# A two-layer diffusion trunk on one core: the opening's mean, context columns and load plan, and the neighbourhood scores in one matmul

## The chip, the cores and the metric

The kernel runs on one core of a Trainium2 chip. The metric is the device time of one execution in microseconds (us), from start to end of the program. A core has engines that run side by side, each with its own queue of instructions: TensorE (PE, matrix multiplies; PEld is its weight load), VectorE (DVE), ScalarE (ACT), GpSimd (POOL) and SyncE (SP), which issues the transfers (DMA) from the main memory. Engines wait for one another by semaphores. Matmuls write to PSUM, eight banks of 512 float32 per partition; everything else lies in SBUF, 128 partitions wide.

## The reference, cut to what matters

```python
for l in range(DEPTH):                                   # DEPTH = 2, D_MODEL = 1024
    mod = silu_c @ w_mod[l] + b_mod[l]                   # 6 vectors of 1024 for the latent tokens
    mod_c = silu_cc @ w_mod[l] + b_mod[l]                # the same for the context tokens
    h = modulate(rms_norm(x, norm1[l]), sh1, sc1)        # 512 latent tokens
    hc = modulate(rms_norm(ctx, norm1[l]), csh1, csc1)   # 256 context tokens
    na_q, na_k, na_v, gq, gk, gv, ga, gb = jnp.split(h @ w_in[l], IN_SPLITS, axis=-1)
    ...                                                  # the same of hc @ w_in[l]
    ya = merge_heads(na_latent(qa, ka, va, ka_c, va_c, bias, row_idx))
    ...                                                  # yb: grouped-query attention
    x = x + g1 * branch_merge(ya, yb, ga, gb, w_pa[l], w_pb[l], w_o[l])
    ...                                                  # the context likewise, but not in the last layer
    h2 = modulate(rms_norm(x, norm2[l]), sh2, sc2)
    x = x + g2 * swiglu(h2, w_ffn_in[l], w_ffn_out[l])
return rms_norm(x, final_norm)

def rms_norm(x, g):
    y = x * lax.rsqrt(jnp.mean(x * x, axis=-1, keepdims=True) + EPS)
    return y * g

def na_latent(q, k, v, k_ctx, v_ctx, bias, row_idx):     # 8 heads, a window of 8 x 16 in a grid of 8 x 64
    s_win = jnp.einsum('bhrwd,bhrjud->bhrwju', qg, kg) * SCALE + bias[None]
    s_ctx = jnp.einsum('bhrwd,bhld->bhrwl', qg, k_ctx) * SCALE
    p = jax.nn.softmax(jnp.concatenate([s_win, s_ctx], axis=-1), axis=-1)
    ...
```

So the softmax of a latent query of the neighbourhood heads runs over its window of latent keys and all 256 context keys.

## The kernel before, in words

All activations are kept with features on the partitions: the 1024 features are eight blocks `k` of 128 partitions (`KB = 8`), and the 768 tokens are columns, 512 latent (`S`) and then 256 context (`T = 768`). Each float32 product is made of three matmuls on rounded halves: high by high, high by low, low by high.

**The opening** (`Trunk.start`, L812 on) computes the first layer's norm and modulation and the first three blocks of the input projection, `gk`, `gv` and `gq`, numbered `i` = 0, 1, 2. It is written as a list of operations with an engine, an estimated cost, what they come after, and an urgency (`Ops.add`). `Ops.run` (L554) puts them in an order by simulating the engines with these estimates, from a start time `START`, and issues them in this order for all engines; on PE, where its own simulation sees a gap, it puts in small matmuls without a use (`warm`, L836). What the list holds:

- `token` and `square`: load block k of x (eight loads, each 128x768), square it on ScalarE.
- `total` (L847): VectorE adds squares 1 to 6 onto square 0, six adds that form a chain; square 7 is kept apart.
- `means` (L853): per 128 tokens one matmul with a column of 1/1024, once for the summed tile and once for square 7, both into `st`.
- `eps`, `power`, `widen`: add epsilon, raise to -1/2 on GpSimd, spread the result over the partitions into `rb` by TensorE (L870).
- `fetch` (L631 in `raw`): the first layer's modulation weights `wmod`, two loads of 512 KB per block k, into nine buffers (`AHEAD`), so that a load from the tenth on waits for an earlier block's sums. `sums` (L891): 16 matmuls per block into a bank of the tag `m`. `parts` (L897): ScalarE copies the bank out. `choose` (L901): four small matmuls that sort the result. `settle` (L906, L909): VectorE finishes the block's scale and shift.
- `scaled`, `high`, `low` (L915, L920, L924): per block and span `s` (0: 512 latent columns, 1: 256 context columns) the modulated norm and its two rounded halves.
- `wraw`, `whigh`, `wlow`: load and split the weights of `gk`, `gv`, `gq` (`win`).
- `multiply` (L950): three matmuls per (i, s, k) into the bank of (i, s). There are three banks of the tag `a`. The banks are taken where a sum begins, so (0, 0), (1, 0), (2, 0) get one each, and a context sum (i, 1) waits until (i, 0) has been copied out: `prev = [out[i, 0]] if s else []`.

PSUM's eight banks in this stage are three for `a`, three for `n` (`ch`, `st`, `rb`) and two for `m`. The order of the loads is the string `FIRST`: the eight blocks of x, the small biases, then `0 w 1 2 w 3 w 4 5 6 7`, where a digit is a block of wmod and `w` a block of win. The loads of the next stage (`mixing`) are not in the list; the build places them into SP's queue by its own simulation.

**Attention** (`mixing`, L1658 on) runs pairs of query blocks as items, with the remaining projections as filler between them. In the first layer the order on PE is written out by `Flow`, from fixed costs per item; in the second layer `Plan` records all operations of all engines and puts them in order by its own simulation, with costs by the width of each operation (`cost`, L351). The latent tokens are sorted so that a block of 128 queries (16 columns of the grid) needs 256 neighbouring latent keys.

**Neighbourhood scores** (`na_pair`, L1424): for each of a head's four query blocks `b` there is one bank `s` of 512 scores: 256 latent keys, then 256 context keys. It is filled by matmuls with `q` as weights (high and low half, `hl`) and `k` as the moving operand: for b < 3 latent keys from 128 b on (256 columns) and the context keys (256). For b = 3 the window wraps around: latent keys 384 to 512 (128 columns), 0 to 128 (128), and the context (256). `soft` (L1441) adds the bias tile from `rpb` and finds the minimum, ACT takes the exponential. `turn` (L1456) transposes the 128x128 pieces for the product with the values; `to` is where a piece lands.

Of the kernel before, what the change touches and what calls it, by code (L numbers as in the profile page):

```python
# [3 lines left out]

# [85 lines left out]
HOWW = "vvv"  # L90
START, HOP, LAND = 4.06, 0.15, 0.25
SAME = dict(v=0.22, a=0.0, g=0.0, p=0.0)
# [511 lines left out]
class Trunk:  # L604
# [207 lines left out]
    def start(self, h, pool, others):  # L812
# [19 lines left out]
        add = todo.add  # L832
        chosen = self.ps("n", "ch")

        def warm():
# [10 lines left out]
        def total(k):  # L846
            nc.vector.tensor_tensor(sqs[0], sqs[0], sqs[k], op=ALU.add)  # L847

        def means(k):
            if k == 0:  # L850
                tiles["st"] = self.ps("n", "st")
            for t in range(nt):
                nc.tensor.matmul(  # L853
                    tiles["st"][:, t : t + 1], sqs[k][:, t * P : (t + 1) * P], self.ones, start=(k == 0 and t == 0),
                    stop=(k > 0), skip_group_check=True)

# [86 lines left out]
        def multiply(i, s, k):  # L943
            if k == 0:
                self.ahead[i, s] = self.ps("a", "pj")
# [11 lines left out]
        for what in FIRST.split():  # L957
            if what == "x":
                k = len(loaded)
                loaded.append(add("d", 0.92, token, (k,), [], 1))  # L960
                sq = add("a", 0.77, square, (k,), [loaded[k]], 1)
                if k < KB - 1:
                    last = add("v", 0.87, total, (k,), [last, sq], 1) if k else sq
                    continue
                last = add("p", 1.34, means, (0,), [last], 0)
                last = add("v", 0.08, eps, (), [add("p", 1.34, means, (KB - 1,), [last, sq], 0)], 0)
                wide = [
                    add("p", c, widen, (s,), [add("g", g, power, (s,), [last], 0)], 0)
                    for s, c, g in ((0, 0.86, 0.96), (1, 0.43, 0.63))]
            elif what == "w":  # L970
                i = len(wdone)
                hi = add("a", 0.97, whigh, (i,), [add("d", 1.26, wraw, (i,), [], 1)], 2.15 + 0.1 * i)
                eng = HOWW[i]
                wdone.append((hi, add(eng, 2.31 if eng == "g" else 1.13, wlow, (i, eng), [hi], 2.15 + 0.1 * i)))
            elif what == "b":
                bias = add("v", 0.35, biases, (), [add("d", 0.45, small, (), [], 1)], 0)
            else:
                k = int(what)
                at = []
                for half in range(2):  # L980
                    at.append(add("d", 1.26, fetch, (k, half), free[-AHEAD] if len(free) >= AHEAD else [], 1))
                    free.append([])
                run = add("p", 1.2, sums, (k,), at, 3 + 0.1 * k)
                for users in free[-2:]:
                    users.append(run)
                run = add("a", 0.4, parts, (k,), [run], 0)
                run = add("p", 0.5, choose, (k,), [run], 0)
                got[k] = add("v", 0.4, settle, (k,), [run, bias], 0)
        for t, n in ((self.cos, "cos"), (self.sin, "sin")):
# [3 lines left out]
        for k in range(KB):  # L993
            for s, (u, hi, lo) in enumerate(((0.68, 0.62, 0.68), (0.4, 0.4, 0.4))):
                t = add("v", u, scaled, (k, s), [wide[s], got[k], loaded[k]], 2 + k * 0.1)
# [3 lines left out]
        for s in range(2):  # L999
            for i in range(3):  # L1000

                prev = [out[i, 0]] if s else []
                for k in range(KB):
                    prev = [add("p", (0.7, 0.37)[s], multiply, (i, s, k), [*halves[k, s], *wdone[i], *prev], 4)]
                out[i, s] = add("a", (1.05, 0.6)[s], evac, (i,), prev, 1)
        everything = {mybir.EngineType[e] if hasattr(mybir.EngineType, "__getitem__") else getattr(mybir.EngineType, e)
# [417 lines left out]
    def na_pair(self, head, q, k, val, bias, out, i, pool, done=None):  # L1424
# [4 lines left out]
        def scores(s, b):  # L1429
            if b < 3:  # L1430
                parts = [(0, 256, P * b)]
            else:
                parts = [(0, P, P * b), (P, 256, 0)]
            parts.append((256, 512, S))
            for hl in range(2):
                for j, (lo, up, src) in enumerate(parts):
                    nc.tensor.matmul(
                        s[:, lo:up], q[hl][:, b * P : (b + 1) * P], k[:, src : src + up - lo],
                        start=(hl == 0 and j == 0), stop=(hl == 1 and j == len(parts) - 1), skip_group_check=True)
# [16 lines left out]
        def turn(c):  # L1456
            tp = self.ps("t", "tp")
            for b in range(2):
                for j in range(2):
                    to = 2 * j + b if c else 2 * b + j  # L1460
                    nc.tensor.transpose(
# [830 lines left out]
    def run(self):  # L2292
# [3 lines left out]
        with (  # L2296
# [7 lines left out]
            self.wpool = _Bufs(wpool, dict(wr=4, wh=3, wl=3))  # L2304
            self.pbufs = dict(a=3, n=3, m=2)
            h = ([], [])
# [115 lines left out]
def kinds(a, b):  # L2422

    return [(f, u, s) for f, u, s in ((a, min(b, S), 0), (max(a, S), b, 1)) if f < u]


# [159 lines left out]
def _layout(a):  # L2586
# [41 lines left out]

    d["rpb"] = np.where(inside, a["na_rpb"][:, :, dr, dc][:, :, :, None], np.float32(-BIG)).reshape(DEPTH, 8, P, 768)
    return {k: c(v) for k, v in d.items()}  # L2630
# [14 lines left out]
```

## Time and profile before

| | |
|---|---|
| median of 3 runs | 1946.68 us (1945.83 to 1948.26) |
| the profiled execution's own time | 1943.38 us |
| its span, first to last instruction | 1940.7 us |
| its granted TensorE clock | 0.998 |
| matmuls (and as many weight loads) | 12300 |
| moved by DMA | 210.85 MB, mean 109 GB/s |

A row of the timeline is: start, duration, engine, line, operation, the tile written and the tiles read, shape, count, and in brackets the idle time before it with what ended it. Consecutive instructions of one kind are one row. A matmul's duration is longer than the time until the next one starts, since matmuls overlap; what a matmul costs in a stream is read from start to start. A row of the windows is: stretch, its length, busy time and instructions of PE, PEld, DVE, ACT, POOL, the granted clock, the share of the DMA engines' time, and GB/s. A row of the chain of work that ended last is start, length, engine, tile, line, count. L540 is the line from which `Plan` issues all operations of the second layer's attention.

### The profile page before, as it was taken

To read this page: it belongs to the slowest core of one execution; us is meant where nothing else is said; L and a number is where in the kernel's file an instruction comes from. 1 tells how busy PE (TensorE), PEld (TensorE's weight loads), DVE (VectorE), ACT (ScalarE), POOL (GpSimd) and SP (SyncE) were. 2 spreads that over 40 slices of the span, in tenths; PEclk is the share of its full clock that TensorE was granted. 3 is DMA by queue.
4 is the path that set the end of the run, shared out by engine and by line. 5 is a ranking of instruction groups with operands and counts; after the bars stand their busy time and mean duration, and the time that the engine had idled before them with its cause. 6 is when DMAs were issued, how large, how long until landed. Compare 5 with 4: busy or idle time off the path is not lost.

```text
span 1940.7 us, 31522 instructions
## 1 busy us (share of the span) xinstructions
PE 1909.2 (98%) x12300; PEld 1764.5 (91%) x12300; DVE 1471.7 (76%) x2797; ACT 937.8 (48%) x1820; POOL 227.5 (12%) x132
## 2 busy tenths in 40 slices
PE   8999999999999999999999999999999999999998
PEld 6989999898889999999999888889988999999998
DVE  6468887769777888787868578898557587877785
ACT  4456666642226533343424345666553355544553
POOL 0432212214300000000000012132210000000000
PEclk9999999999999999999999999999999999999999
DMA  8121112235462134334443411022145532332332
GB/s 328 46 69 42 53 58 63 77 120 179 158 217 87 66 109 130 109 120 131 139 144 131 152 55 33 34 79 82 55 128 175 199 109 77 98 120 90 104 96 83
DMA packets 71670, 210.85 MB, mean 109 GB/s; under 512 B 8545, under 2 KB 10721, under 8 KB 71521
## 3 DMA queue, kind: packets, MB, share of 16 engines
q1 hardware_dynamic: 71520, 208.84, 32.9%
q8 instruction: 96, 1.57, 0.3%
q14 instruction: 54, 0.43, 0.1%
HBM read 196.75 MB, written 6.82 MB: 105 GB/s over the span
## 4 chain that ended last, share of the span: by engine, by line
PE 64%; DVE 5%; issue 1%; ACT 1%; DMA 1%; POOL 0%; SPq 0%; DVEq 0%; POOLq 0%; ACTq 0%
PE po L655 21%; PE qu L2021 14%; PE qv L2021 7%; PE pj L540 4%; PE qc L2021 3%; PE pj L655 3%; PE pf L655 3%; PE pp L655 2%; PE sc L540 2%; PE y L540 2%; PE tp L540 1%; PE pv L540 1%; ACT p L540 1%; DVE m L540 1%; DVE ptl L540 0%
## 5 line engine op out<-in xcount | busy, mean ns | idle before, releaser
L2021 PE MATMUL qu<-r,w 128*128 128x384 f32 (+1 forms) x1872 | 295.9, 310 | 0.3
L2021 PEld LDWEIGHTS qu<-r,w 128*128 128x128 f32 x1872 | 281.0, 189 | 5.0 <-DVE tt L2501 3.8
L1884 ACT ACTIVATE w<-wr 128x512 fp32r<-128x512 f32 x234 | 145.5, 625 | 107.6 <-DVE wr L2465 36.2
L655 PE MATMUL po<-ph,wh 128*128 128x512 f32 (+1 forms) x576 | 197.4, 343 | 0.0
L655 PE MATMUL po<-ph,wl 128*128 128x512 f32 (+1 forms) x576 | 196.8, 342 | 0.0
L655 PE MATMUL po<-pl,wh 128*128 128x512 f32 (+1 forms) x576 | 196.2, 341 | 0.0
L655 PE MATMUL pj<-h,wh 128*128 128x512 f32 (+1 forms) x512 | 182.1, 356 | 1.4 <-DVE ql L1256 1.1
L655 PE MATMUL pj<-h,wl 128*128 128x512 f32 (+1 forms) x512 | 176.8, 345 | 0.9 <-POOL wl L642 0.9
L655 PE MATMUL pj<-hl,wh 128*128 128x512 f32 (+1 forms) x512 | 176.6, 345 | 0.0
L1876 DVE SCALAR_TENSOR_TENSOR x<-po,G,x 128x256 f32<-128x256 f32 (+3 forms) x168 | 99.2, 596 | 100.7 <-PE po L655 99.7
L1888 DVE TENSOR_TENSOR w<-wr,w 128x512 fp32r<-128x512 f32 x234 | 159.3, 685 | 11.3 <-ACT w L1884 10.3
L640 ACT ACTIVATE wh<-wr 128x1024 fp32r<-128x1024 f32 (+1 forms) x109 | 101.3, 933 | 137.2 <-PE po L655 30.4
L2021 PE MATMUL qv<-r,w 128*128 128x384 f32 (+1 forms) x936 | 150.6, 309 | 0.3 <-ACT tt L2027 0.3
L2021 PEld LDWEIGHTS qv<-r,w 128*128 128x128 f32 x936 | 141.2, 190 | 0.5 <-ACT tt L2027 0.5
L782 POOL TENSOR_TENSOR rs<-rs,expo 128x2 f32<-128x2 f32 (+2 forms) x7 | 5.5, 784 | 1099.8 <-DVE rs L781 1099.8
L642 POOL TENSOR_TENSOR wl<-wr,wh 128x1024 fp32r<-128x1024 f32 (+1 forms) x47 | 103.5, 2205 | 229.2 <-ACT wh L640 228.9
L655 PEld LDWEIGHTS po<-ph,wl 128*128 128x128 f32 x576 | 108.2, 188 | 14.4 <-DVE wl L2192 0.4
L655 PEld LDWEIGHTS po<-pl,wh 128*128 128x128 f32 x576 | 108.5, 188 | 12.8
L655 PEld LDWEIGHTS po<-ph,wh 128*128 128x128 f32 x576 | 108.5, 188 | 12.8
L722 DVE CUSTOM_DVE_ANT_0 wr<-wr,crow 128x1024 f32<-128x1024 f32 x80 | 100.2, 1252 | 14.3 <-DMA wr<-wmodT 14.0
L655 PEld LDWEIGHTS pj<-h,wl 128*128 128x128 f32 x512 | 96.8, 189 | 13.4 <-POOL wl L642 1.3
L655 PEld LDWEIGHTS pj<-h,wh 128*128 128x128 f32 x512 | 97.0, 189 | 11.9 <-PE tp L1331 1.1
(341 smaller groups left out, 4705.7 us busy)
## 6 DMA issues: line engine op xcount, KB each, us to landing
wr<-wfi SPq DMA_DIRECT2D x88, 512.0 KB, 3.2
wr<-wmodT SPq DMA_DIRECT2D x80, 512.0 KB, 3.4
wr<-win SPq DMA_DIRECT2D x68, 512.0 KB, 3.7
wr<-wfo SPq DMA_DIRECT2D x64, 256.0 KB, 2.7
wr<-wo SPq DMA_DIRECT2D x26, 512.0 KB, 4.1
wr<-wmod SPq DMA_DIRECT2D x16, 512.0 KB, 9.9
wr<-wp SPq DMA_DIRECT2D x32, 256.0 KB, 2.9
x<-x SPq DMA_DIRECT2D x16, 384.0 KB, 7.1
```

What stands on the lines that cost most here:

```text
L540: ops[i]["run"](*ops[i]["args"], **ops[i]["kw"])
L640: nc.scalar.activation(hi, raw, AF.Copy)
L642: (eng or nc.gpsimd).tensor_tensor(lo, raw, hi[:].bitcast(F32), op=ALU.subtract)
L655: nc.tensor.matmul(ps[:, : b - a], u[:, c], v[k][:, a:b], start=(k == 0 and i == 0), stop=(k == nk - 1 and i == 2),)
L722: self.nc.vector.tensor_tensor_reduce(junk if s else w, w, crow[:, s], 1.0, 0.0, ALU.mult, ALU.add, self.mod[l][:, s, n : n + 1])
L782: nc.gpsimd.tensor_tensor(r[:, :nb], r[:, :nb], self.expo[:, :nb], op=ALU.pow)
L1876: self.nc.vector.scalar_tensor_tensor(x[j][:, f:u], ps[:, f - a : u - a], self.G[l][i][:, s, j : j + 1], x[j][:, f:u], op0=ALU.mult, op1=A ...
L1884: self.nc.scalar.activation(t[:, :n], src, AF.Copy)
L1888: self.nc.vector.tensor_tensor(t[:, n : 2 * n], src, t[:, :n].bitcast(F32), op=ALU.subtract)
L2021: nc.tensor.matmul(banks[bank], u[:, c], v, start=(first and k == 0 and i == 0), stop=(k == kn - 1 and i == 2), skip_group_check=True)
```

## The change

- **Means**: squares are added in pairs (0 and 1, 2 and 3, 4 and 5), three adds without a chain; the means are accumulated on TensorE over five tiles (three pairs, square 6, square 7).
- **Context columns early**: a fourth bank of the tag `a`, taken for (0, 1) from the start, so that the context columns of `gk` need not wait for a bank; in exchange the tag `m` has one bank. (1, 1) then waits for (0, 0) to be copied out, and (2, 1) for (1, 0).
- **Plan**: `START` and several estimated costs of the opening are other numbers.
- **Scores**: for b < 3 one matmul of 512 columns, whose moving operand is read in two runs of 256 (`apart`); for b = 3 two matmuls, 128 columns and 384. For that the latent keys of block 3 change places in the bank (0 to 128 first, then 384 to 512, which lie right ahead of the context keys), and with them the columns of the bias tile and the places in `turn`.

```diff
-START, HOP, LAND = 4.06, 0.15, 0.25
+START, HOP, LAND = 3.9, 0.15, 0.25
...
         chosen = self.ps("n", "ch")
+        for i, s in ((0, 0), (1, 0), (2, 0), (0, 1)):
+            self.ahead[i, s] = self.ps("a", "pj")
...
         def total(k):
-            nc.vector.tensor_tensor(sqs[0], sqs[0], sqs[k], op=ALU.add)
+            nc.vector.tensor_tensor(sqs[k - 1], sqs[k - 1], sqs[k], op=ALU.add)
...
-                    stop=(k > 0), skip_group_check=True)
+                    stop=(k == KB - 1), skip_group_check=True)
...
         def multiply(i, s, k):
-            if k == 0:
+            if (i, s) not in self.ahead:
                 self.ahead[i, s] = self.ps("a", "pj")
...
-                loaded.append(add("d", 0.92, token, (k,), [], 1))
+                loaded.append(add("d", 1.02, token, (k,), [], 1))
                 sq = add("a", 0.77, square, (k,), [loaded[k]], 1)
+                if k % 2 == 0 and k < KB - 2:
+                    even = sq
+                    continue
+                if k < KB - 2:
+                    sq = add("v", 0.87, total, (k,), [even, sq], 1)
+                last = add("p", 1.34, means, (k if k >= KB - 2 else k - 1,), [sq] + ([] if last is None else [last]), 0)
                 if k < KB - 1:
-                    last = add("v", 0.87, total, (k,), [last, sq], 1) if k else sq
                     continue
-                last = add("p", 1.34, means, (0,), [last], 0)
-                last = add("v", 0.08, eps, (), [add("p", 1.34, means, (KB - 1,), [last, sq], 0)], 0)
+                last = add("v", 0.08, eps, (), [last], 0)
...
-                hi = add("a", 0.97, whigh, (i,), [add("d", 1.26, wraw, (i,), [], 1)], 2.15 + 0.1 * i)
+                hi = add("a", 0.97, whigh, (i,), [add("d", 1.25, wraw, (i,), [], 1)], 2.15 + 0.1 * i)
...
-                run = add("p", 1.2, sums, (k,), at, 3 + 0.1 * k)
+                run = add("p", 1.0, sums, (k,), at, 3 + 0.1 * k)
...
-            for s, (u, hi, lo) in enumerate(((0.68, 0.62, 0.68), (0.4, 0.4, 0.4))):
+            for s, (u, hi, lo) in enumerate(((0.58, 0.6, 0.66), (0.39, 0.42, 0.39))):
...
-                prev = [out[i, 0]] if s else []
+                prev = [out[i - 1, 0], out[i, 0]] if s and i else []
                 for k in range(KB):
-                    prev = [add("p", (0.7, 0.37)[s], multiply, (i, s, k), [*halves[k, s], *wdone[i], *prev], 4)]
-                out[i, s] = add("a", (1.05, 0.6)[s], evac, (i,), prev, 1)
+                    prev = [add("p", (0.69, 0.36)[s], multiply, (i, s, k), [*halves[k, s], *wdone[i], *prev], 4)]
+                out[i, s] = add("a", (1.05, 0.6)[s], evac, (i,), prev + ([out[i, 0]] if s else []), 1)
...
             if b < 3:
-                parts = [(0, 256, P * b)]
+                parts = [(s.rearrange("p (a c) -> p a c", c=256), apart(k, P * b, S, 256))]
             else:
-                parts = [(0, P, P * b), (P, 256, 0)]
-            parts.append((256, 512, S))
+                parts = [(s[:, 0:P], k[:, 0:P]), (s[:, P:512], k[:, P * b : T])]
             for hl in range(2):
-                for j, (lo, up, src) in enumerate(parts):
+                for j, (to, keys) in enumerate(parts):
                     nc.tensor.matmul(
-                        s[:, lo:up], q[hl][:, b * P : (b + 1) * P], k[:, src : src + up - lo],
+                        to, q[hl][:, b * P : (b + 1) * P], keys,
                         start=(hl == 0 and j == 0), stop=(hl == 1 and j == len(parts) - 1), skip_group_check=True)
...
-                    to = 2 * j + b if c else 2 * b + j
+                    to = 2 * j + b if c else 2 * b + (j if 2 * i + b < 3 else 1 - j)
...
-            self.pbufs = dict(a=3, n=3, m=2)
+            self.pbufs = dict(a=4, n=3, m=1)
...
+def apart(t, a, b, n):
+
+    near = t[:, a : a + n].unsqueeze(1).to_broadcast([P, 2, n])
+    return replace(near, ap=[near.ap[0], (b - a, 2), near.ap[2]])
...
-    d["rpb"] = np.where(inside, a["na_rpb"][:, :, dr, dc][:, :, :, None], np.float32(-BIG)).reshape(DEPTH, 8, P, 768)
+    rpb = np.where(inside, a["na_rpb"][:, :, dr, dc][:, :, :, None], np.float32(-BIG)).reshape(DEPTH, 8, P, 768)
+    d["rpb"] = np.concatenate([rpb[..., 0:512], rpb[..., 640:768], rpb[..., 512:640]], axis=-1)
```

The string `FIRST` and the number of buffers `AHEAD` stay as they are.

More of the change, by code (lines that the diff above doesn't have):

```diff
@@ L3 @@
 from contextlib import ExitStack
+from dataclasses import replace
 import numpy as np
@@ L975, in start @@
             elif what == "b":
-                bias = add("v", 0.35, biases, (), [add("d", 0.45, small, (), [], 1)], 0)
+                bias = add("v", 0.35, biases, (), [add("d", 0.2, small, (), [], 1)], 0)
             else:
@@ L980, in start @@
                 for half in range(2):
-                    at.append(add("d", 1.26, fetch, (k, half), free[-AHEAD] if len(free) >= AHEAD else [], 1))
+                    at.append(add("d", 1.25, fetch, (k, half), free[-AHEAD] if len(free) >= AHEAD else [], 1))
                     free.append([])
-                run = add("p", 1.2, sums, (k,), at, 3 + 0.1 * k)
+                run = add("p", 1.0, sums, (k,), at, 3 + 0.1 * k)
                 for users in free[-2:]:
                     users.append(run)
-                run = add("a", 0.4, parts, (k,), [run], 0)
-                run = add("p", 0.5, choose, (k,), [run], 0)
-                got[k] = add("v", 0.4, settle, (k,), [run, bias], 0)
+                run = add("a", 0.36, parts, (k,), [run], 0)
+                run = add("p", 0.46, choose, (k,), [run], 0)
+                got[k] = add("v", 0.34, settle, (k,), [run, bias], 0)
         for t, n in ((self.cos, "cos"), (self.sin, "sin")):
```

## The prediction

> **What bounds the kernel now.** I read the page first, then busy time by stages, then the opening as a timeline, engine by engine.
>
> ```profile
> span 1940.7 us, 31522 instructions
> PE 1909.2 (98%) x12300; PEld 1764.5 (91%) x12300; DVE 1471.7 (76%) x2797; ACT 937.8 (48%) x1820; POOL 227.5 (12%) x132
> ```
> ```profile
> 20.00:30.00 10.00, 8.90 (x89) 6.37 (x89) 7.22 (x18) 5.82 (x10) 0.00 (x0) 1.00 1.03 420
> 30.00:40.00 10.00, 8.56 (x74) 4.88 (x73) 8.67 (x20) 4.52 (x9) 0.00 (x0) 1.00 1.03 415
> ```
> ```profile
> 260.00:400.00 140.00, 138.39 (x1021) 129.78 (x1019) 109.61 (x284) 89.19 (x214) 34.39 (x21) 1.00 0.24 72
> ...
> 1310.00:1430.00 120.00, 118.34 (x827) 108.16 (x826) 83.77 (x211) 70.27 (x156) 36.30 (x22) 1.00 0.26 85
> ```
>
> TensorE is busy for 98% of the span, at a granted clock of 1.00 in all four windows. In the two stages with neighbourhood scores (the last two rows) only 1.6 us in each is idle, so a TensorE instruction removed there is time removed. Only the opening is different: from 20 to 40 us the DMA column stands at 1.03 and moves 415 to 420 GB/s, so the loads of the first modulation weights (wmod) set the pace, and PE's busy time there contains filler. These rows of the timeline end its steps, ACT and VectorE first, then PE alone:
>
> ```profile
> 9.14 4.74 ACT L844 ACTIVATE sq<-x 128x768 f32<-128x768 f32 x5 [0.29 <-DMA x<-x]
> ...
> 13.70 0.96 DVE L847 TENSOR_TENSOR sq<-sq,sq 128x768 f32<-128x768 f32 x1
> ...
> 17.85 0.17 DVE L859 TENSOR_SCALAR rs<-st 128x6 f32<-128x6 f32 x1 [3.19 <-PE st L853]
> ...
> 18.88 0.38 ACT L897 ACTIVATE part<-mp 128x256 f32<-128x256 f32 x1 [0.78 <-PE mp L891]
> ```
> ```profile
> 15.07 2.74 PE L853 MATMUL st<-ones,sq 128*128 128x1 f32 x24
> 17.74 1.07 PE L891 MATMUL mp<-wr,cols 128*32 128x256 f32 x16
> 18.74 0.49 PE L836 MATMUL ch<-ident_sb 128*128 128x128 f32 x2
> ...
> 20.61 0.51 PE L901 MATMUL ch<-pick,part 128*128 128x2 f32 x4
> 21.04 1.52 PE L891 MATMUL mp<-wr,cols 128*32 128x256 f32 x24
> 23.07 0.64 PE L891 MATMUL mp<-wr,cols 128*32 128x256 f32 x8 [0.51 <-DMA wr<-wmod]
> 23.64 0.61 PE L901 MATMUL ch<-pick,part 128*128 128x2 f32 x4
> 24.11 0.47 PE L836 MATMUL ch<-ident_sb 128*128 128x128 f32 x2
> 25.17 0.58 PE L901 MATMUL ch<-pick,part 128*128 128x2 f32 x4 [0.59 <-DVE mod L909]
> ...
> 26.41 0.60 PE L836 MATMUL ch<-ident_sb 128*128 128x128 f32 x4
> ...
> 27.94 0.71 PE L836 MATMUL ch<-ident_sb 128*128 128x128 f32 x4
> ...
> 35.49 0.64 PE L891 MATMUL mp<-wr,cols 128*32 128x256 f32 x8 [1.39 <-DMA wr<-wmod]
> ...
> 43.36 0.48 PE L950 MATMUL pj<-h,wh 128*128 128x512 f32 x1
> ...
> 53.00 0.28 PE L950 MATMUL pj<-h,wh 128*128 128x256 f32 x1
> ...
> 61.64 1.40 PE L1062 MATMUL st<-hones,sq 128*128 128x2 f32 x12
> ```
>
> The last square ends at 13.9, the last add at 14.7, the means at 17.8, and the first choose starts at 20.6. From then to the first instruction after the opening, at 61.64, are 41.0 us. The work in them: seven sums at 1.00 (17.74 to 18.74), 7.0; eight chooses at 0.43 (20.61 to 21.04), 3.4; 72 latent multiplies at 0.2295 (42 between 43.36 and 53.00), 16.5; 72 context multiplies at 0.12 (53.00 to 61.64), 8.6. That is 35.5, so **5.5 us of the opening are filler (the L836 rows, 1.8) and waiting**. All 72 context multiplies come last, because no fourth bank is there for them, and from 43.36 on multiplies follow one another without a gap.
>
> **The change, part by part.** *Squares in pairs, means on TensorE.* Three of the six adds go, and 60 means matmuls take the place of 24. They run between 6 and 16 us where PE does nothing but filler, so their 24 to 60 at 0.114 (2.74 over 24) cost nothing; without that cover the 36 more would cost 4.1. The chain behind them gets shorter: after the last square (13.9) comes no add any more (0.8, until 14.7) and one set of means (1.4) in place of two (2.7). The mean is ready 2.1 us earlier. What is late next is the first wmod block and its sums. They ran at 17.74, straight behind the means; the first two wmod loads, in the rows below, go out from 9.13 to 10.4 and land 5.5 us after their issue, so the data is there by 15.9 and the sums can go 1.8 us earlier. So the first choose and the first modulated block come about 1.5 to 2 us earlier. This gain lasts only until the next load is waited for.
>
> *Context columns of the first weight early.* Eight groups of three, 8 x 3 x 0.12 = 2.9 us, can now stand in the gaps, seven of them (2.5 us) before the last block. They cost the same wherever they stand; they gain what they fill. The planner that writes out PE's order puts filler only where it sees a gap, and the last filler stands at 27.94: by its own reckoning PE was full from 28 on, and the gaps that it can fill are those from 20.6 to 28.4. Of the 5.5 us these are 0.5 ahead of 23.07, 1.1 between 24.11 and 25.17, 0.5 at 26.41 and 0.5 at 27.94, 2.6 in all, and some 0.5 more from the earlier start, 3.1. The 1.4 at 35.49 is a wait for wmod that the planner doesn't foresee, and I leave it, with the 1 us of small waits behind it. Context groups need VectorE's products of the context columns in time, and VectorE is 8.67 of 10 busy there; I take 2.8 of the 3.1. Bounds: nothing (if PE merely reaches the wait at 35.49 sooner and has done no more) and 5.5 (no gap left).
>
> *Loads.* Their list does not change, but SP's queue holds something that the list doesn't (the first row from the list of DMA issues between 8 and 12 us, the others from SP's timeline):
>
> ```profile
> wr<-wmod SPq DMA_DIRECT2D x2, 512.0 KB, 5.5
> ```
> ```profile
> 9.13 1.29 SPq L631 DMA_DIRECT2D wr<-wmod  x2
> ...
> 18.26 3.92 SPq L631 DMA_DIRECT2D wr<-wmod  x3
> 23.05 1.62 SPq L631 DMA_DIRECT2D wr<-win  x2
> 25.57 5.28 SPq L631 DMA_DIRECT2D wr<-wmod  x5
> ```
>
> Two weights of the next stage stand ahead of the last five wmod loads. At one load every 1.26 us (18.26 to 23.05 to 25.57) they put these off by 2.5 us. That place is decided when the program is built, and earlier means may move it. I take it as unchanged; bounds: 2.5 us sooner, or a third such weight, 1.3 us later.
>
> *Fourth bank, one bank less for the sums.* A sums then waits until ACT has copied the one before: 0.38 us, against 2.5 us between two blocks. Nothing, unless two blocks pile up; then PE stands 0.5 and the multiplies queued behind it with it.
>
> *Scores in one matmul.* In each layer 8 heads x 2 halves have three query blocks with 256+256 columns, now 512, and one with 128+128+256, now 128+384.
>
> ```profile
> 276.11 0.40 PE L1437 MATMUL sc<-k,ql 128*128 128x256 f32 x2
> 276.35 0.51 PE L1437 MATMUL sc<-k,qh 128*128 128x128 f32 x3
> 276.69 0.50 PE L1437 MATMUL sc<-k,ql 128*128 128x128 f32 x3
> 277.03 0.28 PE L655 MATMUL pj<-h,wh 128*128 128x256 f32 x1
> ```
> ```profile
> 662.62 6.24 PE qu L2021 x36
> ...
> 1131.93 10.92 PE pj L655 x48
> ...
> 1363.43 8.64 PE pv L540 x72
> ```
>
> From start to start, two of 256 take 0.24, three (128, 128, 256) take 0.34. One of 512 takes 10.92/48 = 0.2275, one of 384 takes 6.24/36 = 0.173, one of 256 takes 8.64/72 = 0.12, so one of 128 takes (0.34 - 0.12)/2 = 0.11 and the new pair 0.283. Saved: 96 x 0.0125 = 1.2 us and 32 x 0.057 = 1.8 us, **3.0 together**. These stages have some idle time of their own, so I carry 2.8. Bounds: 0, if other engines' order takes it back, and 3.1. A matmul that reads two runs stands nowhere in this trace; I take the row of 512 in one run, to which it is nearest, and keep a doubled 0.455 as the far end.
>
> The Trainium skill ("TensorE: Matmul & The Clock Gate", Back-to-back issue gap) gives N/2.4 plus 2.5 ns for a matmul, so 128 matmuls fewer would save only 0.3 us by it. The rows speak against it here: 128 columns take 0.11, far above its 0.056.
>
> The bias tile's changed order and the transposes' changed places move the same bytes: nothing.
>
> Sum: opening -2.8, scores -2.8, together **-5.6 us**. The profiled execution took 1943.4 (span 1940.7 and 2.7 around it) and would come to 1937.8. The runs shown have a median of 1946.7, which is 3.3 above it; from the median I get **1941.1**. What can be told from no change is about 0.2%, 3.9 us: faster is below 1942.8, slower above 1950.6.
>
> **The rivals.**
>
> *A: the opening's stall only moves.* PE comes to the sums of the sixth block earlier, waits for the same load at 35.49, and the planned order has put the same multiplies ahead of it. For it: the loads run without a pause, and the largest single wait, 1.39, is for them. Against it: the 72 context multiplies stand behind everything now, and each one put ahead of a wait is off the end. It gives -2.8, **1943.9**. 0.24.
>
> *B: the loads come sooner.* With sums earlier, SP no longer places the two weights ahead of wmod; the wait of 1.4 and the 1 us behind it go as well, the opening gains 5.2. For it: the place is the result of a build in which the sums were late. Against it: the buffers for those two weights are free early in either version. -8.0, **1938.7**. 0.18.
>
> *C: slower: the operand in two runs.* If it streams at half the rate, 96 matmuls cost 0.455 in place of 0.24, +20.6; the 32 still save 1.8, the opening 2.8: +16.0, **1962.7**. It turns the whole to a loss from (1.8 + 2.8)/96 = 0.048 us above the 0.24 of the two that it replaces. Against it: each run is 256 columns long, with one jump between. 0.06.
> The Trainium skill ("PSUM — Partial Sum Buffer", Specifications (TRN2)) says that any non-contiguous access pattern slows matmuls significantly, which would be this case; but it says so of PSUM, and the output here is one unbroken row of 512. No row of before shows it for an operand that is read.
>
> *D: it is given back.* The second layer's attention is planned anew with other costs, and the other engines' queues of the first are ordered anew; if new stalls of 5.6 us come of it, nothing is left. For it: VectorE is busy for 78% of the first layer's score stage (109.61 of 140). Against it: the two score stages now hold 3.3 us of idle time in 260, so the new ones would have to be nearly twice all that stands there. **1946.7**. 0.07.
>
> **How the numbers follow.** The forecast, 1941.1, has 0.45, with a range of its own of 1939.5 to 1943.0. Below 1942.8 lie most of it (0.43), B (0.18) and a quarter of A (0.06): faster 0.67. Same: the rest of the forecast and A (0.20) and most of D (0.06), 0.26. Slower: C and a hundredth of D, 0.07. The range runs from 1936.5 (B with both parts at their best: -5.5 - 3.1, and 1.5 for the spread of the runs) to 1946.8 (D); C and what lies beyond the ends are left out, under 2 in 10.
>
> **What would show it.** Right: in the changed kernel the mean's eps starts near 15.7 in place of 17.85; the first choose is 1.5 to 2 us earlier; multiplies of 256 columns stand between 22 and 40 us; no filler after 24; the first L1062 instruction stands near 58.8 in place of 61.64, and the score stages have 128 matmuls fewer, of 512 and 384 columns at 0.23 and 0.17. A would show as a longer wait before the sixth block's sums and an end near 61.6; B as SP rows with all wmod ahead of win; C as scores of 512 that stand 0.29 or more apart; D as an opening that ends early and new PE waits later. The prediction is wrong if the opening ends later than 61.6, or if the layers after the scores take longer than before.

## The result, and the profile after

The changed kernel takes 1951.36 us (median of 22 runs, 1946.29 to 1955.75), the kernel before 1945.23 on the same chip (22 runs, 1940.5 to 1953.08). The ratio is **1.0027 [1.0019, 1.0034]**: some 5 us slower, where 5.6 us faster was forecast, and outside the range that was given. The profiled execution took 1952.35 us.

From its page, the span and the engines' busy time:

```profile
span 1950.5 us, 31244 instructions
...
PE 1913.8 (98%) x12174; PEld 1764.5 (90%) x12174; DVE 1474.9 (76%) x2794; ACT 938.5 (48%) x1820; POOL 227.9 (12%) x132
```

TensorE has fewer instructions and is busy longer than before. Read as windows (busy us of PE, PEld, DVE, ACT and POOL, then the granted clock, DMA share and GB/s), the opening shows a first difference:

```profile
10.00:20.00 10.00, 10.00 (x79) 9.52 (x82) 3.09 (x7) 4.35 (x5) 0.69 (x1) 0.77 1.04 410
20.00:30.00 10.00, 10.00 (x102) 7.21 (x91) 6.03 (x15) 4.11 (x8) 1.91 (x2) 0.89 1.03 421
30.00:40.00 10.00, 10.00 (x87) 6.83 (x84) 9.37 (x22) 5.58 (x11) 0.00 (x0) 1.00 1.03 416
```

PE is busy without a gap, but at a mean granted clock of 0.77 and 0.89 where the profile of before had 1.00. By single microseconds the clock is 0.50 for 6.8 us in a row, from 15.5 to 22.3:

```profile
16.00:17.00 1.00, 1.00 (x7) 1.00 (x6) 0.00 (x0) 0.09 (x1) 0.00 (x0) 0.50 1.03 422
...
20.00:21.00 1.00, 1.00 (x13) 0.19 (x3) 0.36 (x1) 0.05 (x1) 1.00 (x1) 0.50 1.06 434
```

What PE does there, from its timeline, then the last squares on ScalarE, and on VectorE the last add of a pair and the instruction that ends the mean:

```profile
9.73 1.40 PE L856 MATMUL st<-ones,sq 128*128 128x1 f32 x12
...
11.52 1.40 PE L856 MATMUL st<-ones,sq 128*128 128x1 f32 x12
...
13.31 5.71 PE L856 MATMUL st<-ones,sq 128*128 128x1 f32 x36
18.95 1.93 PE L894 MATMUL mp<-wr,cols 128*32 128x256 f32 x16
...
23.19 0.51 PE L904 MATMUL ch<-pick,part 128*128 128x2 f32 x4
...
61.23 1.40 PE L1069 MATMUL st<-hones,sq 128*128 128x2 f32 x12
```
```profile
8.95 3.76 ACT L847 ACTIVATE sq<-x 128x768 f32<-128x768 f32 x4 [0.26 <-DMA x<-x]
12.90 0.84 ACT L847 ACTIVATE sq<-x 128x768 f32<-128x768 f32 x1 [0.19 <-DMA x<-x]
```
```profile
11.79 0.96 DVE L850 TENSOR_TENSOR sq<-sq,sq 128x768 f32<-128x768 f32 x1 [1.01 <-ACT sq L847]
...
19.06 0.17 DVE L862 TENSOR_SCALAR rs<-st 128x6 f32<-128x6 f32 x1 [5.42 <-PE st L856]
```

The mean is ready at 19.06, not at 15.7 as forecast, and later than the 17.85 of before. The first choose comes at 23.19 (20.61 before). Still the opening ends at 61.23, 0.4 us sooner. So in this profile the loss stands behind the opening. Times from the first grouped score (`sc<-kk`) to the last transpose of z (`tp<-ident_sb,z`), read off PE's timeline:

| us | before | after |
|---|---|---|
| start to end of the opening | 61.6 | 61.2 |
| first layer, attention | 312.4 | 317.1 |
| between the two | 784.3 | 784.9 |
| second layer, attention | 249.8 | 253.7 |
| from there to the last means | 496.2 | 497.2 |

Both attention stages became longer, by 4.7 and 3.9 us, though their score matmuls became cheaper, as these rows show:

```profile
272.26 0.39 PE L1443 MATMUL sc<-k,ql 128*128 128x512 f32 x1
272.49 0.40 PE L1443 MATMUL sc<-k,qh 128*128 128x512 f32 x1
...
277.52 0.45 PE L1443 MATMUL sc<-k,qh 128*128 128x128 f32 x2
277.81 0.45 PE L1443 MATMUL sc<-k,ql 128*128 128x128 f32 x2
```

From start to start, 512 columns take 0.23 and the pair of 128 and 384 takes 0.29: the prices of the forecast, and the operand in two runs costs nothing. Waits of PE, and windows at half clock, took it back. The list of waits gives engine, tile, releaser, us in total, times and the longest. First the first layer's stage after, then the second layer's, before and after:

```profile
PE pj L656 <- DVE ql L1263: 2.7, 2, 1.7
PE pv L1229 <- DVE ql L1263: 1.7, 1, 1.7
```
```profile
PE tp L540 <- DVE z L540: 1.2, 1, 1.2
```
```profile
PE tp L541 <- DVE z L541: 3.0, 2, 2.0
PE tp L541 <- DVE p L541: 2.4, 1, 2.4
```

In the first layer the waits for ql were 1.1 and 0.5 before, 2.8 less. There the change also has two windows of 3.4 us at half clock, from 169.1 and from 373.9, where before has none; such a window does 1.7 us less work than one at full clock. So 2.8 of waits and 3.4 of clock, less the 1.5 that the matmuls save, make the 4.7. In the second, VectorE's timeline beside GpSimd's (POOL) and PE's shows what p and z wait for:

```profile
1308.57 2.33 DVE L541 TENSOR_SCALAR p<-p,rc 128x768 f32<-128x768 f32 x1
1310.83 0.15 DVE L541 RECIPROCAL rc<-m 128x1 f32<-128x1 f32 x1
1311.01 2.82 DVE L541 TENSOR_SCALAR p<-p,rc 128x768 f32<-128x768 f32 x1
...
1424.05 4.28 DVE L541 TENSOR_SCALAR z<-z,rc 128x512 f32<-128x512 f32 x2
```
```profile
1308.10 2.38 POOL L541 TENSOR_TENSOR wl<-wr,wh 128x1024 fp32r<-128x1024 f32 x1
1310.83 2.34 POOL L541 TENSOR_TENSOR wl<-wr,wh 128x1024 fp32r<-128x1024 f32 x1 [0.35 <-ACT wh L541]
...
1423.73 1.84 POOL L541 TENSOR_TENSOR bias<-bias 128x768 f32<-128x768 f32 x1
1425.52 2.53 POOL L541 TENSOR_TENSOR wl<-wr,wh 128x1024 fp32r<-128x1024 f32 x1
```
```profile
1313.89 0.44 PE L541 MATMUL tp<-ident_sb,p 128*128 128x128 f32 x2 [2.43 <-DVE p L541]
...
1428.39 0.55 PE L541 MATMUL tp<-ident_sb,z 128*128 128x128 f32 x2 [1.98 <-DVE z L541]
```

A scaling of p with 768 columns takes 0.62 when GpSimd is idle (this one is from the experiment scores_only):

```profile
1309.17 0.62 DVE L541 TENSOR_SCALAR p<-p,rc 128x768 f32<-128x768 f32 x1
```

Here each of the two that begin while GpSimd works ends 0.4 to 0.7 us after GpSimd's instruction, and takes 2.33 and 2.82. In the trace of before the first of the same two began later within GpSimd's first split and the second fell between the splits:

```profile
1303.76 1.39 DVE L540 TENSOR_SCALAR p<-p,rc 128x768 f32<-128x768 f32 x1
1305.08 0.15 DVE L540 RECIPROCAL rc<-m 128x1 f32<-128x1 f32 x1
1305.26 0.62 DVE L540 TENSOR_SCALAR p<-p,rc 128x768 f32<-128x768 f32 x1
```
```profile
1302.35 2.38 POOL L540 TENSOR_TENSOR wl<-wr,wh 128x1024 fp32r<-128x1024 f32 x1
1306.02 2.39 POOL L540 TENSOR_TENSOR wl<-wr,wh 128x1024 fp32r<-128x1024 f32 x1 [1.28 <-PE sc L540]
```

And behind the wait of 1.98 PE's clock is at half for over 3 us (windows of the kernel after):

```profile
1429.00:1430.00 1.00, 1.00 (x3) 0.73 (x3) 1.00 (x3) 0.96 (x2) 0.00 (x0) 0.50 0.00 0
1430.00:1431.00 1.00, 1.00 (x7) 0.98 (x5) 0.82 (x4) 1.00 (x4) 0.00 (x0) 0.50 0.00 0
...
1432.00:1433.00 1.00, 1.00 (x9) 0.92 (x9) 0.36 (x3) 0.69 (x2) 0.00 (x0) 1.00 0.84 309
```

### The profile page after: what moved, and what is told of

Read it like the earlier page. It is cut to its first block, busy times and chain, and to the rows that moved or that the text cites. A ratio compares the mean times of both kernels' runs of the same rounds, so it can differ in the third digit from the quotient of the medians.

```text
span 1950.5 us, 31244 instructions
## 1 busy us (share of the span) xinstructions
PE 1913.8 (98%) x12174; PEld 1764.5 (90%) x12174; DVE 1474.9 (76%) x2794; ACT 938.5 (48%) x1820; POOL 227.9 (12%) x132
## 4 chain that ended last, share of the span: by engine, by line
PE 63%; DVE 6%; issue 2%; ACT 1%; DMA 1%; POOL 0%; SPq 0%; DVEq 0%; POOLq 0%; ACTq 0%
PE po L656 20%; PE qu L2027 13%; PE qv L2027 7%; PE pj L541 4%; PE qc L2027 3%; PE pj L656 3%; PE pf L656 3%; PE pp L656 2%; PE y L541 2%; PE sc L541 1%; PE tp L541 1%; PE pv L541 1%; DMA wr<-wmodT 1%; DVE m L541 1%; ACT p L541 1%
## 5 line engine op out<-in xcount | busy, mean ns | idle before, releaser
L656 PEld LDWEIGHTS pj<-h,wh 128*128 128x128 f32 x512 | 98.0, 191 | 15.5 <-DVE ql L1263 2.0
```

The costliest lines, as they stand in the source:

```text
L656: nc.tensor.matmul(ps[:, : b - a], u[:, c], v[k][:, a:b], start=(k == 0 and i == 0), stop=(k == nk - 1 and i == 2),)
```

## The experiments

Twelve kernels, in three groups that each ran on one chip beside the kernel before. "Stage 1" and "stage 2" are the attention stages of the table above, from each kernel's profile; the clock is the mean of the granted clock over all runs of the kernel.

| kernel | ratio to before | clock | opening ends | stage 1 | stage 2 |
|---|---|---|---|---|---|
| after | 1.0027 [1.0019, 1.0034] | 0.9933 | 61.2 | 317.1 | 253.7 |
| open_only | 1.0013 [1.0000, 1.0025] | 0.9938 | 62.5 | 312.3 | 250.4 |
| scores_only | 1.0000 [0.9990, 1.0009] | 0.9953 | 63.3 | 314.4 | 251.4 |
| means_adds | 0.9987 [0.9976, 0.9999] | 0.9951 | 62.3 | 314.8 | 249.6 |
| means_warm | 1.0026 [1.0012, 1.0040] | 0.9960 | 64.0 | 314.4 | 253.1 |
| context_only | 0.9998 [0.9986, 1.0010] | 0.9960 | 61.7 | 312.4 | 249.7 |
| means_only | 1.0012 [1.0001, 1.0022] | 0.9936 | 62.2 | 312.1 | 249.8 |
| scores_l1 | 1.0009 [0.9998, 1.0021] | 0.9951 | 61.8 | 312.1 | 254.7 |
| best | 1.0001 [0.9990, 1.0011] | 0.9958 | 61.7 | 313.9 | 253.7 |
| after_port | 0.9998 [0.9989, 1.0007] | 0.9935 | 63.0 | 315.7 | 247.8 |
| adds_port | 0.9973 [0.9961, 0.9984] | 0.9961 | 61.6 | 314.8 | 246.6 |
| best_port | 0.9980 [0.9971, 0.9989] | 0.9961 | 61.4 | 312.8 | 248.3 |
| before_port | 0.9985 [0.9976, 0.9995] | 0.9956 | 60.9 | 314.0 | 249.0 |

Before stands at a clock of 0.9954 to 0.9958, 61.6, 312.4 and 249.8. A stage of one profile holds a half-clock window or none by chance of the run (1.7 us), so the ratios decide and the stages say where. The profile of before was one with few such windows (clock 0.998, against 0.9954 to 0.9958 over the runs), and its span is 9.8 us shorter than the change's where the ratio says 5.3. The opening's end scatters too: the same opening as before's ends at 60.9, 61.6, 61.8 and 63.3 in before_port, before, scores_l1 and scores_only.

**open_only**: the change with the scores of before.

```diff
-                parts = [(s.rearrange("p (a c) -> p a c", c=256), apart(k, P * b, S, 256))]
+                parts = [(0, 256, P * b)]
...
+            parts.append((256, 512, S))
```

> The changed kernel with the scores as before (three matmuls per pair again). Theory: the opening's gain was eaten by the TensorE clock, which falls to 0.50 while PE does little but one-column means, and the later loss comes from the scores edit alone. So here the clock is 0.50 from about 15 to 22 us, the opening ends near 61.2 us (0.4 sooner than before), no wait in the score stages is longer than before (longest 1.2), and the time is within 2 us of before (ratio 0.999 to 1.001). Rival 1, the loss starts in the opening and its shift brings half-clock windows later: about as slow as the changed kernel, ratio 1.002 to 1.0035. Rival 2, chance alone: half-clock windows come and go from run to run, and all four kernels of this call spread over each other.

1.0013, between what the theory and rival 1 expected, and the opening ends at 62.5, not near 61.2. The opening's part alone brings no gain, and its clock between 10 and 20 us is 0.72. The longest of its later waits for z or p is 1.1, as the theory said. That the other 0.0014 comes with the scores is likely, but the two intervals overlap.

**scores_only**: the kernel before with the scores of the change (with the bias columns and the transposes' places that go with them).

```diff
-                parts = [(0, 256, P * b)]
+                parts = [(s.rearrange("p (a c) -> p a c", c=256), apart(k, P * b, S, 256))]
...
-            parts.append((256, 512, S))
```

> The kernel before with the scores edit alone. Theory: 128 matmuls fewer give 3.0 us, but VectorE's and ScalarE's queues come out in another order in both score stages, so that PE waits 1.5 us or more in several places (for ql, for z, for p), and each such wait brings a window of 3.4 us at clock 0.50. Opening as before, clock 1.00, ending at 61.6; waits of the score stages 4 us or more above before; time 3 to 6 us above before, ratio 1.0015 to 1.003. Rival 1 (the loss starts in the opening): 3 us faster than before, ratio 0.9985. Rival 3, the operand read in two runs is slow: matmuls of 512 columns in the scores stand 0.29 us or more apart; theory: 0.23.

1.0000: neither the loss of 3 to 6 us that the theory expected nor the gain of rival 1. Of the 3.0 us of matmuls that are saved nothing is left. Its waits for z in the second layer are 3.3 us in place of 1.2.

**means_adds**: the change with the six adds and two sets of means of before.

```diff
-                if k % 2 == 0 and k < KB - 2:
-                    even = sq
-                    continue
...
+                    last = add("v", 0.87, total, (k,), [last, sq], 1) if k else sq
```

> The changed kernel with the means as before (six adds on VectorE, two sets of means); early context columns, fourth bank and scores stay. Theory: the clock stays at 1.00 in the opening, context columns fill gaps, and the opening ends between 58.6 and 60.0 us in place of 61.2; the score stages lose as in the changed kernel, so the time is 1.5 to 3 us below the changed kernel's and still above before. If the clock had no part in the opening: no gain over the changed kernel, or 1 us worse because the mean is later.

0.9987: undoing this one part turns the loss of 0.0027 into a gain, more than was expected. But the opening ends at 62.3, not between 58.6 and 60.0, so the gain doesn't come in the way that was expected.

**means_warm**: the change with one filler matmul behind each matmul of the means; the planner's cost of a set is 2.2 in place of 1.34.

```diff
                     stop=(k == KB - 1), skip_group_check=True)
+                warm()
```

> The changed kernel with one small filler matmul of 128 columns behind each of the 30 means matmuls. Theory: the filler keeps the clock at 1.00 through 15 to 22 us; the mean's eps starts near 16.5 in place of 19.06 in spite of 0.9 us of filler in its last set; the opening ends between 57.8 and 59.5 in place of 61.2, and the time is 2 to 3.5 us below the changed kernel's. If filler does not hold the clock: eps later than 19 and the opening not earlier than 61.

Its windows in the opening:

```profile
10.00:20.00 10.00, 10.00 (x91) 10.00 (x91) 3.56 (x6) 4.87 (x6) 0.00 (x0) 1.00 1.04 410
20.00:30.00 10.00, 9.49 (x104) 7.42 (x103) 1.89 (x8) 2.35 (x5) 1.69 (x2) 1.00 1.03 421
```

With 128 columns of filler between them the same means keep the clock at 1.00, which speaks for the row of one-column matmuls as what loses it. The time did not follow: a pair of one mean and one filler takes 0.445 us (10.22 to 10.66), the sums start only at 23.27, and the ratio stays at 1.0026. So much filler costs time of its own, and that a full clock would win the lost time is not shown by this run.

**context_only**: fourth bank, early context and the new plan numbers on the kernel before; means and scores are those of before.

```diff
+        for i, s in ((0, 0), (1, 0), (2, 0), (0, 1)):
+            self.ahead[i, s] = self.ps("a", "pj")
...
-            self.pbufs = dict(a=3, n=3, m=2)
+            self.pbufs = dict(a=4, n=3, m=1)
```

> The kernel before with the fourth bank, the early context multiplies and the new plan numbers; means and scores as before. Theory M (the means on TensorE cost the time): without them the prediction's 2.8 us come, about -2.5 us, ratio 0.9985 to 0.999; the first choose near 20.6 as before, the opening ends near 59 in place of 61.6, and the granted clock stays at 1.00 from 10 to 30 us. Rival P (the new plan costs it: early multiplies stand in the way of sums): the opening ends at 62 or later with the clock at 1.00, ratio 1.001 or above.

Neither: 0.9998, an opening that ends at 61.7, and no 2.5 us. The first choose came at 23.4 and a half-clock window began at 20.2, though no means were added on TensorE. The timeline has only six context multiplies (two groups of the eight) ahead of the last choose, in this kernel and in the change. Here they even took the place of three latent ones, of which 27 in place of 30 stand ahead of it, so that the way from the last choose to the end is 18.57, as long as the 18.64 of before. VectorE, which makes the operands, is full there:

```profile
30.00:40.00 10.00, 10.00 (x95) 6.47 (x87) 9.93 (x22) 5.25 (x10) 0.00 (x0) 1.00 1.03 415
```

**means_only**: the means on TensorE alone, on the kernel before.

```diff
-            nc.vector.tensor_tensor(sqs[0], sqs[0], sqs[k], op=ALU.add)
+            nc.vector.tensor_tensor(sqs[k - 1], sqs[k - 1], sqs[k], op=ALU.add)
```

> The kernel before with pairs of squares and four sets of means on TensorE; three banks, late context, old plan numbers and old scores. Theory M: the granted clock falls to 0.50 for one or two windows between 15 and 23 us, the eps comes at 18.5 to 19.5, the first choose 2 us or more after the 20.6 of before, and the time rises by 3 to 5 us, ratio 1.0015 to 1.0026. Rival P: the clock stays, eps comes near 17.4 or earlier, and the ratio is 1.000 or below.

1.0012, or 2.3 us, with a clock of 0.76 and 0.90 between 10 and 30 us, the eps at 18.68 and the first choose at 22.84. Theory M holds, with a price somewhat below the expected 3 to 5 and hardly clear of nothing.

**scores_l1**: the scores in one matmul in the second layer alone; the planner still counts the old matmuls, so that the order on every other engine is that of before.

```diff
+            if not plan:
+                for hl in range(2):
+                    for j, (lo, up, src) in enumerate(old):
...
+                        "tensor", "matmul", merged if j == len(old) - 1 else (lambda *a, **kw: None),
```

> The scores in one matmul in the second layer alone, with the plan computed as for the old matmuls, so that the queues of VectorE, ScalarE, GpSimd and SyncE stand exactly as before; the first layer and the opening are those of before. Theory O (what the edit saves is taken back by the other engines' new order): here half of the 3.0 us comes out, -1 to -1.5 us, ratio 0.9992 to 0.9995, and the stretch of the second layer's score stage is 1.5 us shorter. Rival W (TensorE only reaches the same waits sooner, whatever the order): no change, ratio 1.000, with PE's waits in that stage longer by what is saved.

Theory O falls: with the queues exactly as before, stage 2 takes 254.7 in place of 249.8, and the ratio is 1.0009. It isn't the order, it is when things meet:

```profile
1309.83 0.44 PE L541 MATMUL tp<-ident_sb,p 128*128 128x128 f32 x2 [2.43 <-DVE p L541]
```

The same wait of 2.43 as in the change, and again both scalings of p lie under GpSimd's splits, 2.33 and 2.82 long. Rival W is only half right: PE doesn't merely meet old waits. GpSimd's work there starts with an operation on the bias tile that waits for a load, and it starts at 1302.24 in place of 1300.56, while VectorE's first scaling comes only 0.75 later than before.

**best**: context_only with scores_l1, and the last square's set of means ahead of the sum's.

```diff
-            if k == 0:
+            if k == KB - 1:
                 tiles["st"] = self.ps("n", "st")
```

> What the runs so far speak for: early context with the fourth bank and the new plan numbers, means by six adds on VectorE as before but with the last square's set of means put ahead of the sum's set, and the scores in one matmul in the second layer alone with the queues of before. Theory M with O: eps near 16.9 in place of 17.85, opening near 58 to 59, second layer's score stage 1.5 us shorter: -4 us, ratio 0.998. Rivals P and W: 1.000 or above.

1.0001: the gain of 4 us didn't come. The mean was quicker in both kernels with this edit (17.67 here, 16.92 in best_port), and the openings end at 61.7 and 61.4: an earlier mean alone buys nothing. The expected 1.5 us of stage 2 went as in scores_l1, the wait for p being 2.45.

From here on theory L: a scaling on VectorE that meets GpSimd's split stands still until that ends, TensorE waits, and the wait is followed by a window at half clock. The test takes four scalings, found by their place in VectorE's queue, to ScalarE, and leaves every other instruction in place:

```diff
+                if (to.name[0], seen[to.name[0]]) in ASIDE:
+                    Engines.last.scalar.activation(to, of, AF.Copy, scale=r[:, 0:1])
+                    continue
```

**after_port**:

> The changed kernel in which four scalings of the second layer (the 29th and 30th of p, the 25th and 26th of z), which stood on VectorE beside GpSimd's weight splits, run on ScalarE; every other instruction keeps its place. Theory L (while GpSimd runs its split VectorE's scaling stands still, TensorE waits for it, and a wait of some 2 us is followed by a window at half clock): the 2.4 wait for p goes, the 3.0 for z falls to 1 or less, the half-clock window near 1428 goes, the second layer's score stage (from its first score to its last transpose) takes 249 to 251 in place of 254.0, ratio 1.0003 to 1.0013 in place of 1.0027. Rival N (TensorE meets the next late thing, ScalarE's queue among them): stage above 253, ratio 1.002 or more.

0.9998 in place of 1.0027, stage 2 at 247.8, below what was expected. Its waits in that stage:

```profile
PE sc L551 <- ACT p L551: 1.2, 4, 0.5
PE tp L551 <- ACT z L549: 1.0, 2, 0.8
```

The waits for VectorE's p and z are gone, the longest wait that is left is 0.94 for kk, which every kernel has, and no window at half clock is left in the stage. The moves also shift GpSimd's second split, which starts 2.9 us after its first has ended; that is part of the effect. Four other scalings, which meet no split, were not moved for comparison, so that some of the gain could come from a shorter queue of VectorE.

**adds_port**, **best_port** and **before_port**: the same four moves on means_adds, best and before.

> The changed kernel with the six adds and two sets of means of before, and the same four scalings on ScalarE. Theory L: the wait for z, 3.3, falls to 1 or less, the half-clock window near 1420 goes, the stage takes 246 to 248 in place of 250.0, ratio 0.9965 to 0.998. Rival N: as that kernel without the move, ratio 0.9987 or more.

> Early context, adds on VectorE with the last square's means first, scores in one matmul in the second layer alone, and the four scalings on ScalarE. Theory L: the wait for p and the half-clock window between 1300 and 1320 go, the stage takes 248 to 250 in place of 254.0, ratio 0.998 or below in place of 1.0001. Rival N: 1.000.

> The kernel before with nothing but the four scalings on ScalarE. There the two scalings of z took 1.63 and 1.85 and TensorE waited 1.2 for them; those of p cost TensorE nothing. Theory L: -1 us, ratio 0.9994, stage 249 in place of 250.2. Rival N: 1.000 or above.

0.9973, 0.9980 and 0.9985: theory L three times, and rival N falls. The kernel before gains more than expected, 2.9 us for 1: its stage got 0.8 shorter in the profile, and where the rest of that came from I did not trace. adds_port and best_port are faster than both kernels of the case; adds_port is the change without its means on TensorE and with four scalings moved.

## Why the prediction was wrong, point by point

The step that failed most is a term put at nothing: the means on TensorE, which cost 2.3 to 7.8 us in four pairs of kernels. The two gains of 2.8 failed as well. The last group gives the sum in steps. Moving the scalings gains 0.0029 (5.6 us) on the change and 0.0015 (2.9) on the kernel before, so the meeting of VectorE and GpSimd costs the change **2.7 us more**. After_port against adds_port, which differ in the means alone: **4.9 us for the means on TensorE**. The other pairs with this one difference give 7.8 (the change and means_adds), 2.9 (open_only and context_only) and 2.3 (means_only and before). Adds_port against before_port, early context and scores where the meeting is out of the way: **a gain of 2.3**, where 5.6 was forecast for the whole change. Together 2.7 + 4.9 - 2.3 = 5.3, the loss that was measured. The steps come from one chain of ratios, so that they add up proves nothing by itself, and each is uncertain by 2 to 3 us: the 2.7 and the 2.3 alone are hardly clear of nothing.

*Means on TensorE cost nothing, mean ready 2.1 us earlier: wrong, and the largest error.* I counted the 36 more matmuls as hidden beside the squares, and the last set alone behind the last square. A set takes 1.4 on PE, but the inputs of the last three sets are ready within 1.1 us: square 6 at 12.71, the last pair's sum at 12.75, square 7 at 13.74. So the sets pile up, and their 36 matmuls stand in one row from 13.31. At 0.114 each this is 4.1 us, until 17.4, hardly before the 17.85 of before. At half clock it was 5.71. Means_warm shows that the clock went with these matmuls, and over all runs the four kernels with bare means on PE stand at 0.9933 to 0.9938, all others at 0.9951 to 0.9961. That is 0.002 of 1945, or 4 us at full clock lost, two windows' worth. In the opening the four profiles with bare means have 6.8 or 10.2 us at half clock up to 24.7 us; of the nine with adds six have 3.4 and three none, so half clock is not absent with the adds either. But how the lost clock becomes lost time stays open. The profiles place only 1.4 us of the 4.9 in the opening (63.0 against 61.6), which is within the scatter of openings, and the change's own opening is not later at all; in stage 1 the change and after_port also wait 1.7 and 2.0 for ql before pv, where adds_port waits 0.6. What connects that wait with the means I did not find out.

The Trainium skill ("TensorE: Matmul & The Clock Gate", What's actually happening) has the clock fall to half after an idle window of about 3.4 us that runs freely. The windows here are of that length, but PE's rows are full (1.00 of 1.00 us busy) while it falls: here a row of matmuls of one column did not keep the clock up.

*Context groups early, 2.8: wrong.* I bounded it by the gaps on PE, and named VectorE's load as the risk. Two groups of eight came early, 0.7 us; VectorE was full there, though no run shows what a freer VectorE would have given. From the last choose to the end of the opening PE has no gap, and how long this takes follows from the multiplies that are left: the change takes 17.9 us (43.31 to 61.23) for 42 latent and 66 context ones, the kernel before 18.65 (42.99 to 61.64) for 42 and 72.

*The opening's gain, and rival A.* A was right in its core: the opening's end doesn't follow the mean. The last wmod load is issued by 30.8 in both kernels; SP's row after:

```profile
24.28 6.56 SPq L632 DMA_DIRECT2D wr<-wmod  x6
```

The last choose stands at 42.99 before and 43.31 after, with first chooses 2.6 us apart. That the two weights ahead of the wmod loads set this end is read from rows; a kernel with those loads behind was not tried. My step "loads unchanged" was right, and I should have drawn the conclusion from it. The 1.26 us per load that I read there holds from 23.05 to 25.57; from 18.26 on it is 1.5, which changes no term. Rival B didn't happen.

*Fourth bank, nothing: right.* No wait for the sums' one bank shows in the change. In means_warm, where everything is later, PE waits 0.5 for it once, as long as I said for two blocks that pile up.

*Scores, 2.8: the price right, the step to time wrong.* 0.23 and 0.29 are the forecast's 0.2275 and 0.283, and rival C is out. The 0.056 that I set against the rows' 0.11 is not contradicted by them: the Trainium skill ("TensorE: Matmul & The Clock Gate", Back-to-back issue gap) gives this formula for an isolated matmul and says that it counts too little at small sizes where weights are loaded. But I carried 2.8 of 3.0 to the end because PE had 1.6 us of idle time in a stage, and that says how much slack PE has, not how much VectorE has. In the second layer the saving let PE, VectorE and GpSimd meet otherwise: 4.2 us more of waits for p and z and one window of 1.7, against 1.5 saved. In the first, the wait for ql before pj grew from 0.2 to 1.8 in scores_only and means_adds alike, about the 1.5 that the stage's matmuls save; there VectorE's queue has ql behind other work. That this order is the cause was not tested by itself, and in the second layer the like theory fell.

*Rival D, "it is given back": the right one, at 0.07.* I let it end at no change, since new stalls of 5.6 us seemed many beside 3.3 of idle time. They were new stalls in kind, not more of the old: PE's wait of 2.43 for p was nowhere in the trace of before. Yet that trace held the sign, in the same two scalings of z (VectorE, then GpSimd):

```profile
1415.50 1.63 DVE L540 TENSOR_SCALAR z<-z,rc 128x512 f32<-128x512 f32 x1
...
1417.24 1.85 DVE L540 TENSOR_SCALAR z<-z,rc 128x512 f32<-128x512 f32 x1
```
```profile
1414.45 2.39 POOL L540 TENSOR_TENSOR wl<-wr,wh 128x1024 fp32r<-128x1024 f32 x1 [0.75 <-ACT wh L540]
1416.79 2.02 POOL L540 TENSOR_TENSOR bias<-bias 128x768 f32<-128x768 f32 x1
```

One operation of one shape with a duration that varies from 0.49 to 1.85 is a meeting that a shift of 1 to 2 us can make worse.

## What to carry to other kernels

Work moved to TensorE "beside other work" is free only if its pieces come no faster than TensorE takes them; compare the two periods, and count the pile behind the last one. Where an operation's duration varies for one shape, ask what runs beside it before shortening anything near it: a saving of 1.5 us in a full stage is easily less than one new meeting of two engines. Where a stage's end stays put while its first half moves, look first for a load or another engine's queue that sets it.

## What the runs showed of the hardware

*VectorE and GpSimd.* A scaling in SBUF that starts under GpSimd's split, or under its operation on a bias tile, lasts until 0.2 to 0.7 us after that has ended: 0.62 becomes 2.33 and 2.82, two of 0.49 become 4.28. Under GpSimd's operation on a tile of 128x8 (hr, from 1194.09 to 1195.72 in the kernel before) two scalings of p took 0.62 all the same. The Trainium skill ("SBUF — State Buffer", Who interferes with whom) says that such VectorE operations and GpSimd share a port pair as an exclusive lock, so that the later one blocks for the other's whole instruction. The rows of the splits and bias operations agree, those of hr don't show it, and moving four scalings gave 2.7 to 5.6 us in four kernels.

*The clock after short waits.* Six kernels have a wait of 1.98 us or more for p or z in the second layer's stage (after, scores_only, means_adds, means_warm, scores_l1, best). Each has half clock there, 3.4 us long (6.8 in scores_only), which begins within such a wait or up to 1.3 us behind it. The eight profiles without such a wait have none in that stage. It does not follow every one of them: after and means_warm have two such waits and one window each. Nor does it need one: near 170 us five profiles have such a window, where PE waits 0.6 in all. So with a wait of some 2 us in a stream that is otherwise full there often came a window at half clock, which is worth up to 1.7 us more.
